# Delta rule in a streaming encoder: decay products moved ahead, write strengths in the exponent, joining products with the identity and 32x32 tiles, more buffers and banks

## The chip, the cores and the metric

The kernel runs on one core of one Trainium2 chip. The metric is the device time of one execution in microseconds (us), the median of several runs. A smaller number is better.

## The reference

One inference step of a two-layer encoder over 2048 prompt tokens and 32 sample tokens (model width 1024, all float32). Layer one is a gated delta rule with 8 heads of 128; layer two is windowed attention, which the change does not touch. What matters here is the delta rule in blocks of c tokens:

```python
gcum = jnp.cumsum(gb, axis=-1)
decay = jnp.exp(jnp.where(incl, gcum[..., :, None] - gcum[..., None, :], -jnp.inf))
kbeta = kc * bc[..., None]
lower = jnp.where(strict, jnp.einsum('nbhik,nbhjk->nbhij', kbeta, kc) * decay, 0.0)
tmat = lower + jnp.eye(c, dtype=lower.dtype)
u = lax.linalg.triangular_solve(tmat, vc * bc[..., None], left_side=True, lower=True, unit_diagonal=True)
w = lax.linalg.triangular_solve(tmat, kbeta * jnp.exp(gcum)[..., None], left_side=True, lower=True,
                                unit_diagonal=True)
intra = jnp.einsum('nbhik,nbhjk->nbhij', qc, kc) * decay
...
v_new = ui - jnp.einsum('bhck,bhkv->bhcv', wi, s)
o = jnp.einsum('bhck,bhkv->bhcv', qd, s) + jnp.einsum('bhij,bhjv->bhiv', ai, v_new)
s = s * gl[..., None, None] + jnp.einsum('bhck,bhcv->bhkv', kd, v_new)
```

The output o is normalised per head, multiplied by a gate from z, projected by `a_w_out`, added to the input and layer-normalised.

## The kernel before

The engines are TensorE (PE, with PEld for its weight loads), VectorE (DVE), ScalarE (ACT) and GpSimd (POOL); transfers are issued by SyncE (SP) and a few by ACT. Tokens lie in 5 blocks of 416. The stages follow each other:

- **P1** projects the tokens to q, k and v (each float32 product as three passes over high and low parts), applies the short convolution, and stores q, k, v and the running sums of the decay (`gcum`) in scratch memory. `gates` and `norms` make small tables for each token and head: `cc` (write strength times a norm), `ekd`, `egl`, `hn`, `rq` and `ngc` (minus the running sum).
- **Delta.run** walks over 17 chunks: 16 of 128 tokens and one of the 32 sample tokens. In between it gives PE other work in small portions (`fill`): the remaining blocks of the gate z while i is under 7, and the first tiles of the output projection once i is 15.
- **O1** projects 17 tiles of up to 128 tokens with `a_w_out`; `second.rest()` does what is left of them after the chunks. Then come **P2** (projections of layer two) and **Attention**.

In iteration i of Delta.run four chunks are in work: `ch` (chunk i), `nx` (i+1), `n2` (i+2) and `n3` (i+3). The steps of a chunk, each a generator that is advanced piece by piece:

- `load`: SP fetches `gb` (the running sums spread over all partitions), `k`, `q`, `v`, and later `z`, each in two halves of four heads. `gb` has four buffers, that is two chunks' worth, so `gb` of n3 is written over that of nx.
- `decays` (of n3): DVE adds the causal mask to `gb` (E, line 417), ACT takes eight exponentials (L423), DVE multiplies by `cc` (L427).
- `lower` (of n2): PE forms k times k (tile `g`, L441), DVE multiplies by E (`npr`), ACT gathers the 32x32 diagonal blocks, DVE transposes them into `L` (L451).
- `chain`: forward substitution inside the 32x32 blocks, 31 steps of one multiplication (tile `tm`, L462) and one subtraction (`Tt`, L465). Steps 0 to 23 run on POOL one iteration ahead, the rest on DVE (`SPLIT = 24`).
- `spread` and `invert` (of nx): DVE transposes the result, ACT spreads it into `t32` and `u32`, and five small products with copies between them (all called `bps`, in one PSUM bank) join the 32x32 inverses to a 128x128 one, `u`. The fourth product (L575) needs `ta`, which DVE makes from the third (L571).
- `turn_k`, `turn_v`, `inside`: transposes of k and v, and q times k times E. `inside` also lets ACT turn `gb` into powers (L507).
- `fade` (of nx): DVE multiplies the two halves of k, and then of q, by those powers (L516). After it `gb` of nx is free.
- `errors`, `changes`, `seen`, `advance`: k times state S (`ks`), `u` times the error (`vp`, copied to `vs`), the output (`op`), and the new state (`sp`, then S on DVE, L638).
- `squares`, `norms`, `scale`, `emit`: the normalisation, the transpose `otr`, and the product with z that is stored as `s_g`.

Within `Delta.run` the order on PE, DVE and ACT is that of the code (`tc.manual_schedule`). The order on SP and POOL, and that of all engines outside it, is set by the framework's planner. Each engine works strictly in its order, so an instruction that waits holds all behind it. In `second.rest()` only PE's order is that of the code.

Of the kernel before, what the change touches and what calls it, by code (L numbers as in the profile page):

```python
# [10 lines left out]
F32 = mybir.dt.float32  # L11
# [84 lines left out]
class P1:  # L96
# [49 lines left out]
    def qkv(self):  # L146
        nc, I, T, G, big, one = self.nc, self.I, self.T, self.G, self.big, self.one
        gtmp = one.tile([128, 8, NTT, H], F32, tag="gtmp", name="gtmp")
        abT = gtmp[:, 0:2].rearrange("p a t h -> p (a t h)").rearrange("p (t c) -> p t c", c=16)
# [97 lines left out]
def gates(nc, I, T, G, abT, gtmp, one, pt):  # L247
# [28 lines left out]
    V.reciprocal(out=G["cc"][:], in_=w)  # L276
# [27 lines left out]

def norms(nc, G, parts, sel, kind, one, pt):
# [17 lines left out]
    V.tensor_tensor(out=G["cc"][:], in0=G["cc"][:], in1=xv, op=ALU.mult)  # L323
    V.tensor_tensor(out=G["ekd"][:], in0=G["ekd"][:], in1=G["cc"][:], op=ALU.mult)
# [32 lines left out]
class Delta:  # L357
# [3 lines left out]
    SPLIT = 24  # L361

    def __init__(self, tc, es, I, O, T, G):
# [15 lines left out]
        self.f = {}  # L379
        for k in ("t32", "u32", "m1"):  # L380
            self.f[k] = one.tile([128, 8, 64], F32, tag=k, name=k)
        nc.gpsimd.memset(self.f["m1"][:], 0.0)
# [6 lines left out]
        self.S = one.tile([128, 8, 128], F32, tag="Sp", name="Sp")  # L389
        nc.gpsimd.memset(self.S[:], 0.0)  # L390
# [19 lines left out]
    def decays(self, ch):  # L410
# [13 lines left out]
        yield  # L424
        for q in range(2):
            E = ch.E[q]
            V.tensor_tensor(out=E[:n, :, :n], in0=E[:n, :, :n], in1=self.bc(G["cc"][:n, ti, q * 4:q * 4 + 4], n, n),  # L427
                            op=ALU.mult)
            yield

    def lower(self, ch):
# [4 lines left out]
        nb = self.sml.tile([128, 8, 32], F32, tag="y1", name="nb")  # L436
# [58 lines left out]
    def inside(self, ch):  # L495
# [3 lines left out]
        for q in range(2):  # L499
# [19 lines left out]
    def corners(self, ch):  # L519
        m1, npr = self.f["m1"], ch.npr  # L520
        self.nc.scalar.copy(m1[0:32, :, 32:64], npr[0:32, :, 32:64])
        self.nc.scalar.copy(m1[64:96, :, 32:64], npr[64:96, :, 96:128])

    def spread(self, ch):

        nc, V = self.nc, self.nc.vector
        n = ch.n
        sml = self.sml
        both = sml.tile([128, 2, 8, 32], F32, tag="ta", name="tcp")
        tcf, ucp = both[:, 0], both[:, 1]  # L530
        V.transpose(tcf[:n].rearrange("q p (c d) -> q c d p", d=4), ch.Tt[:n].rearrange("q i c -> q c i"))
        V.transpose(ucp[:n], tcf[:n])
        if n == 32:
            V.tensor_copy(self.u[:32, :, :32], ucp[:32])
            return
        t32, u32 = self.f["t32"], self.f["u32"]
        for dst, src in ((t32, tcf), (u32, ucp)):
            for c in range(2):
                nc.scalar.activation(dst[:, :, 32 * c:32 * c + 32], src[:], AF.Copy, scale=self.sides[:, c:c + 1])

    def invert(self, ch):
# [5 lines left out]
        t32, u32, m1, npr = self.f["t32"], self.f["u32"], self.f["m1"], ch.npr  # L547
        halves = (slice(0, 64), slice(64, 128))

        def new():  # L550
            return self.pb.tile([128, 8, 64], F32, tag="tr", name="bps")

        y1p = new()
# [10 lines left out]
        for hv in halves:  # L564
            V.tensor_tensor(out=u[hv, :, hv], in0=u32[hv], in1=up[hv], op=ALU.subtract)
        yield
        tp = new()
# [978 lines left out]
```

## Time and profile before

| What | Value |
|---|---|
| median of 3 runs | 2457.42 us (2456.83 to 2467.69) |
| profiled execution, its own time | 2461.63 us |
| its span | 2459.8 us |
| PE busy | 2251.2 us (92%) |
| DVE busy | 1441.0 us (59%) |
| ACT busy | 875.9 us (36%) |
| POOL busy | 781.3 us (32%) |
| Delta.run with its neighbours | from about 700 to 1380 us in the span |

The page gives one profiled execution. Busy shares are averages over stages that differ: PE is near 100% in P1, P2 and Attention, and lower in the chunk loop. The stage is read by windows, by the waits in it, and by the instructions in order of time.

### The profile page before, as it was taken

How to read it: one execution, taken by the hardware profiler on the slowest of the kernel's cores; microseconds unless marked ns; L12 is line 12 of the kernel's file. 1: busy time of each engine (PE TensorE's matmuls, PEld its weight loads, DVE VectorE, ACT ScalarE, POOL GpSimd, SP SyncE). 2: the span in 40 equal slices, each digit the busy share in tenths (PEclk: the TensorE clock that was granted, in tenths of full speed). 3: DMA queues.
4: the chain of work that ended last, by engine and by line, in shares of the span. 5: the costliest groups of instructions: out<-in, count | busy, mean ns of one | idle time of the engine just before them, and what ended most of it. 6: DMA issues, size and time to landing. Idle time of an engine off the chain costs nothing.

```text
span 2459.8 us, 36690 instructions
## 1 busy us (share of the span) xinstructions
PE 2251.2 (92%) x13778; PEld 2052.3 (83%) x13778; DVE 1441.0 (59%) x2883; ACT 875.9 (36%) x2133; POOL 781.3 (32%) x1184
## 2 busy tenths in 40 slices
PE   8999999999988888687777899999999998999997
PEld 6999999999977777576676677899999996777885
DVE  3775666544356667687675677622444225767875
ACT  3444344233124445355453211131111225544541
POOL 1422222111104353444452011012434123565653
PEclk9999999999988888888888999999999999999999
DMA  4121212212253443554432566442212247333321
GB/s 177 61 79 70 74 65 73 75 61 97 92 126 81 94 100 92 132 124 118 91 84 71 150 196 190 122 132 87 73 66 74 73 121 183 110 96 94 95 74 56
DMA packets 268592, 247.78 MB, mean 101 GB/s; under 512 B 67600, under 2 KB 243792, under 8 KB 265072
## 3 DMA queue, kind: packets, MB, share of 16 engines
q1 hardware_dynamic: 259456, 233.70, 32.8%
q10 hardware_dynamic: 8960, 11.76, 1.5%
q8 instruction: 108, 1.77, 0.3%
q14 instruction: 68, 0.56, 0.1%
HBM read 154.57 MB, written 91.20 MB: 100 GB/s over the span
## 4 chain that ended last, share of the span: by engine, by line
PE 72%; DMA 10%; DVE 10%; ACT 3%; issue 2%; POOL 1%; SPq 0%; DVEq 0%; ACTq 0%; POOLq 0%
PE ps L77 15%; PE ps L79 15%; PE ps L78 14%; DMA gb<-s_gcum 5%; PE ot L1286 3%; PE po L1171 2%; PE po L1172 2%; PE po L1173 2%; PE S L1265 2%; PE po L877 2%; PE po L879 2%; PE po L878 2%; DMA act_raw<-s_hT 1%; PE tr L1280 1%; PE g L441 1%
## 5 line engine op out<-in xcount | busy, mean ns | idle before, releaser
L77 PE MATMUL ps<-act_hi,w_hi 128*128 128x416 f32 x2000 | 714.9, 358 | 4.1 <-ACT act_hi L68 2.4
L79 PE MATMUL ps<-act_hi,w_lo 128*128 128x416 f32 x2000 | 706.4, 354 | 0.6 <-DVE w_lo L54 0.6
L78 PE MATMUL ps<-act_lo,w_hi 128*128 128x416 f32 x2000 | 705.4, 353 | 0.0
L77 PEld LDWEIGHTS ps<-act_hi,w_hi 128*128 128x128 f32 x2000 | 379.0, 190 | 10.8 <-ACT act_hi L68 3.8
L79 PEld LDWEIGHTS ps<-act_hi,w_lo 128*128 128x128 f32 x2000 | 379.1, 190 | 7.1 <-DVE w_lo L54 1.2
L78 PEld LDWEIGHTS ps<-act_lo,w_hi 128*128 128x128 f32 x2000 | 379.9, 190 | 4.3 <-issue 0.4
L54 POOL TENSOR_TENSOR w_lo<-w_raw,w_hi 128x1024 fp32r<-128x1024 f32 x55 | 144.6, 2630 | 656.3 <-ACT w_hi L53 646.4
L188 DVE SCALAR_TENSOR_TENSOR y<-R,convw,y 128x2083 f32<-128x2083 f32 x72 | 171.6, 2384 | 121.1 <-ACT y L186 119.8
L462 POOL TENSOR_TENSOR tm<-L,Tt 128x60 f32<-128x60 f32 (+21 forms) x384 | 125.4, 327 | 325.9 <-DVE tm L462 207.6
L1273 POOL TENSOR_TENSOR P<-P,sm 128x384 f32<-128x384 f32 (+2 forms) x128 | 104.6, 839 | 158.6 <-DVE sm L1150 86.6
L465 POOL TENSOR_TENSOR Tt<-Tt,tm 128x60 f32<-128x60 f32 (+21 forms) x384 | 140.3, 365 | 30.1
L1146 ACT ACTIVATE P<-S,nm 128x192 f32<-128x192 f32 (+2 forms) x260 | 105.0, 421 | 88.2 <-DVE nm L1139 41.4
L218 ACT COPY R<-ps 128x416 f32<-128x416 f32 (+1 forms) x144 | 61.5, 450 | 209.4 <-PE ps L79 184.3
L53 ACT CAST w_hi<-w_raw 128x1024 fp32r<-128x1024 f32 x62 | 65.0, 1049 | 178.0 <-PE ps L78 147.2
L1011 POOL TENSOR_TENSOR rs<-rs,sin 128x416 f32<-128x416 f32 x50 | 71.0, 1420 | 149.8 <-DVE rs L1010 102.3
L877 PE MATMUL po<-wo_hi,g_hi 128*128 128x512 f32 (+1 forms) x272 | 113.5, 417 | 2.0 <-ACT g_hi L863 1.2
L879 PE MATMUL po<-wo_hi,g_lo 128*128 128x512 f32 (+1 forms) x272 | 109.8, 404 | 3.4 <-DVE g_lo L864 3.4
L878 PE MATMUL po<-wo_lo,g_hi 128*128 128x512 f32 (+1 forms) x272 | 109.2, 401 | 0.0
L575 PE MATMUL bps<-ta,npr 64*64 64x64 f32 x256 | 29.0, 297 | 83.3 <-DVE ta L571 83.3
L1286 PE MATMUL ot<-pt,vd 128*128 128x256 f32 x372 | 98.6, 391 | 3.7 <-DVE graw L1289 1.6
L1171 PE MATMUL po<-wo_hi,g_hi 128*128 128x512 f32 x240 | 99.7, 415 | 0.1
L1172 PE MATMUL po<-wo_lo,g_hi 128*128 128x512 f32 x240 | 96.5, 402 | 2.6 <-DVE wo_lo L824 2.5
(266 smaller groups left out, 4168.1 us busy)
## 6 DMA issues: line engine op xcount, KB each, us to landing
w_raw<-in_w_in SPq DMA_DIRECT2D x40, 512.0 KB
w_raw<-in_b_w_in SPq DMA_DIRECT2D x20, 512.0 KB
s_z<-z SPq DMA_DIRECT2D x40, 208.0 KB
s_bz<-za SPq DMA_DIRECT2D x40, 208.0 KB
s_bq<-ra SPq DMA_DIRECT2D x40, 208.0 KB
s_q<-y SPq DMA_DIRECT2D x8, 1024.0 KB
s_k<-y SPq DMA_DIRECT2D x8, 1024.0 KB
s_v<-y SPq DMA_DIRECT2D x8, 1024.0 KB
```

Source lines behind the costliest of these rows:

```text
L54: sub.tensor_tensor(out=lo[:], in0=raw[:], in1=hi[:], op=ALU.subtract)
L77: nc.tensor.matmul(ps, hi[:, k, :], xh[:, k, :], start=(k == 0), stop=False)
L78: nc.tensor.matmul(ps, hi[:, k, :], xl[:, k, :], start=False, stop=False)
L79: nc.tensor.matmul(ps, lo[:, k, :], xh[:, k, :], start=False, stop=(k == KC - 1))
L188: nc.vector.scalar_tensor_tensor(out=y[:], in0=R[:, j:j + W], scalar=self.convw[:, i, j:j + 1], in1=y[:], op0=ALU.mult, op1=ALU.add)
L465: P.tensor_tensor(out=Tt[:n, i0:, :w], in0=Tt[:n, i0:, :w], in1=tm[:n, i0 - k:, :w], op=ALU.subtract)
L877: nc.tensor.matmul(ps[:n], ghi[:, k, :n], w[0][:, k, cs], start=(k == 0), stop=False)
L878: nc.tensor.matmul(ps[:n], ghi[:, k, :n], w[1][:, k, cs], start=False, stop=False)
L879: nc.tensor.matmul(ps[:n], glo[:, k, :n], w[0][:, k, cs], start=False, stop=(k == KC - 1))
L1171: nc.tensor.matmul(ps[:n], ghi[:, k, :n], w[0][:, k, cs], start=(k == 0), stop=False)
L1172: nc.tensor.matmul(ps[:n], ghi[:, k, :n], w[1][:, k, cs], start=False, stop=False)
L1286: nc.tensor.matmul(ot[:, p], self.vd[:, kc0 + j, p, :], pt[:, 2 * j:2 * j + 2, :], start=(j == 0), stop=(j == nj - 1))
```

## The change

It has these parts:

1. **Write strength in the exponent.** `add_log` computes the logarithm of `cc` in 20 small DVE instructions at the end of the norms of k, and adds it to `ngc`. The exponential of `decays` then holds the factor, and the two multiplications L427 for each chunk go.
2. **Decay products moved ahead.** The powers become a generator of their own (`powers`), and `fade` of nx runs from the end of iteration i-1 into the start of iteration i, before POOL's chain is started. `gb` of n3 is requested behind it as before. `decays` of n3 is advanced in smaller pieces.
3. **Joining products.** `corners` and `t32` go. The first product is 32x32 on the blocks themselves; `y1` is a fixed tile with the identity on its diagonal, so that the second and third products need no addition or subtraction. Product three comes before product two, and their banks alternate between the pools `pa` and `pb`. `ta` is copied by ACT; `u` is copied half by ACT, half by DVE.
4. **Split.** POOL does steps 0 to 24 of a full chunk (25 of 31), and 10 for the sample chunk.
5. **Buffers.** The state S becomes two tiles of four heads; q has five buffers and the v/z tiles three. For the sample chunk the stored state is loaded ahead into buffers of `gb` instead of into S after S was stored. `triu`, `ones` and `cc` live in P1's pools only.
6. **Output weights.** The low parts of `a_w_out` are made by POOL instead of DVE (`wo_lo`), one piece in each iteration from i = 8 on, instead of two.
7. **Planner.** `second.rest()` now keeps the code's order on DVE too.

```diff
+def add_log(nc, out, x, one, n, w):
...
+    V.tensor_scalar(out=ei, in0=xi, scalar1=23, scalar2=None, op0=ALU.logical_shift_right)
+    V.tensor_scalar(out=mi, in0=xi, scalar1=0x7FFFFF, scalar2=0x3F800000, op0=ALU.bitwise_and, op1=ALU.bitwise_or)
...
+    V.tensor_tensor(out=out, in0=out, in1=r[:], op=ALU.add)
...
-    SPLIT = 24
+    @staticmethod
+    def split(ch):
+        return 25 if ch.n == 128 else 10
...
-        pool, tag, bufs = (self.sml, "vz", 2) if name in "vz" else (self.four, name, 4)
+        pool, tag, bufs = (self.sml, "vz", 3) if name in "vz" else (self.four, name, 5 if name == "q" else 4)
...
             nc.scalar.activation(E, E, AF.Exp, bias=G["ngc"][:n, ti, h:h + 1])
-        yield
-        for q in range(2):
-            E = ch.E[q]
-            V.tensor_tensor(out=E[:n, :, :n], in0=E[:n, :, :n], in1=self.bc(G["cc"][:n, ti, q * 4:q * 4 + 4], n, n),
-                            op=ALU.mult)
-            yield
+            if h % 4 == 3:
+                yield
...
-            eg = ch.gb[q][:, :, :n]
-            nc.scalar.activation(eg, eg, AF.Exp)
...
+    def powers(self, ch):
+
+        for gb in ch.gb:
+            eg = gb[:, :, :ch.n]
+            self.nc.scalar.activation(eg, eg, AF.Exp)
+        yield
...
         for p in range(8):
-            for hv in halves:
-                nc.tensor.matmul(y1p[hv, p, :], m1[hv, p, :], t32[hv, p, :], start=True, stop=True)
-        y1 = sml.tile([128, 8, 64], F32, tag="y1", name="y1")
-        nc.scalar.copy(y1[:], y1p[:])
+            for r in (0, 64):
+                s, t = slice(r, r + 32), slice(r + 32, r + 64)
+                nc.tensor.matmul(y1p[t, p, 0:32], npr[s, p, t], ch.tcf[s, p, :], start=True, stop=True)
+        for r in (slice(32, 64), slice(96, 128)):
+            nc.scalar.mul(y1[r, :, 0:32], y1p[r, :, 0:32], -1.0)
         yield
-        up = new()
+        tp = new(self.pa)
+        for p in range(8):
+            nc.tensor.matmul(tp[:64, p, :], u32[:64, p, :], y1[:64, p, :], start=True, stop=True)
+        ta = sml.tile([128, 8, 64], F32, tag="ta", name="ta")
+        nc.scalar.copy(ta[:64], tp[:64])
+        yield
+        up = new(self.pb)
...
-        for hv in halves:
-            V.tensor_tensor(out=u[hv, :, hv], in0=u32[hv], in1=up[hv], op=ALU.subtract)
+        nc.scalar.copy(u[0:64, :, 0:64], up[0:64])
+        V.tensor_copy(u[64:128, :, 64:128], up[64:128])
...
-            go(z, low, low)
+            go(low, x, low)
             if n2:
                 self.load(n2, "v", (0,))
-            go(vp, vp, x, x, t, t, t, t, low, z, t, t, low)
+            go(vp, vp, z, x, z, x, low, t, t, low, t)
             if n2:
-                drain(self.chain(n2, P, 0, self.SPLIT))
+                drain(self.chain(n2, P, 0, self.split(n2)))
             if n3:
                 self.load(n3, "gb")
+            elif n2:
+                S = self.sampled()
...
+            if i > 7:
+                side()
+            if i == len(chunks) - 3:
+                side()
...
-                self.between(ch)
+                self.save("p_delta")
+                self.S = S
...
-            go(w, e, x, x)
+            go(w, e)
...
-            go(v, r, r, r, g, r, r, r, v, d, r, d, r)
+            p = gen(self.powers, n2)
+            go(v, r, r, r, g, r, r, v, r, k, r, d, v, w, r, d, p)
...
-            go(d, d, o)
-            side()
+            go(o)
             fill(more)
-            go(v, o)
+            go(v, o, d)
             z, x = self.emit(ch), gen(self.fade, n2)
+            go(x)
...
-        nc.vector.tensor_tensor(out=lo[:, k, :], in0=raws[k][:], in1=hi[:, k, :], op=ALU.subtract)
+        nc.gpsimd.tensor_tensor(out=lo[:, k, :], in0=raws[k][:], in1=hi[:, k, :], op=ALU.subtract)
...
-    with tc.manual_schedule(engines={ET.PE}):
+    with tc.manual_schedule(engines={ET.PE, ET.DVE}):
         second.rest()
```

What the change does to the order is shown at three places, in an iteration without filler work (i from 8 on).

On DVE before, from the fades of q to the first mask addition of n3 (at: q times k times E; Xo, ro_y and ro_t: the normalisation in small steps; u: the second joining product):

```order
L516 TENSOR_TENSOR q<-q,gb 128x512 x2
L505 TENSOR_TENSOR at<-gq,E 128x512
L654 TENSOR_TENSOR Xo<-Xo,t_rq 128x8
L656 SCALAR_TENSOR_TENSOR Xo<-Xo,t_rq 128x8
L658 TENSOR_SCALAR Xo<-Xo 128x8
L505 TENSOR_TENSOR at<-gq,E 128x512
L331 TENSOR_SCALAR ro_y<-Xo 128x8
L334 TENSOR_SCALAR ro_y<-ro_y 128x8
L338 SCALAR_TENSOR_TENSOR ro_t<-Xo,ro_y 128x8
L565 TENSOR_TENSOR u<-u_5060,bps 64x8x64 x2
L417 TENSOR_TENSOR E<-gb,nm 128x512
```

The first E comes here nine rows behind the fades that its buffer waits for.

On DVE after, the start of the iteration: the fades of nx alternate with `npr` of n2 and the z products, and stand ahead of the transpose L that starts POOL's chain.

```order
L550 TENSOR_TENSOR k<-k,gb 128x512
L471 TENSOR_TENSOR npr<-g,E 128x512
L550 TENSOR_TENSOR k<-k,gb 128x512
L471 TENSOR_TENSOR npr<-g,E 128x512
L709 TENSOR_TENSOR z<-otr,z 128x512
L550 TENSOR_TENSOR q<-q,gb 128x512
L709 TENSOR_TENSOR z<-otr,z 128x512
L550 TENSOR_TENSOR q<-q,gb 128x512
L491 TENSOR_TENSOR tm<-L,Tt 128x6x7
L494 TENSOR_TENSOR Tt<-Tt,tm 128x6x7
L480 STREAM_TRANSPOSE L<-nb 128x1024
```

The four fades moved from the middle of the previous iteration to this place.

And on DVE after, the place of the mask additions of the same iteration:

```order
L369 TENSOR_TENSOR ro_t<-ro_t,ro_y 128x8
L450 TENSOR_TENSOR E<-gb,nm 128x512
L599 COPY u<-bps 64x8x64
L519 TENSOR_TENSOR vn<-vtr,t_hn 128x512
L371 SCALAR_TENSOR_TENSOR ro_y<-ro_t,ro_y 128x8
L450 TENSOR_TENSOR E<-gb,nm 128x512
```

Between the last fade of q and the first E stood nine rows before; now 29 stand there (rows of the change's own list, with groups of four counted once), `ta` is gone from behind E, and one copy of u stands behind the first E.

On SP before, one iteration: `gb` stands behind both loads of k and the first of z; it overwrites what the fades of q read.

```order
L681 DMA s_g<-z 128x4x128
L407 DMA v<-s_v 128x4x128
L681 DMA s_g<-z 128x4x128
L407 DMA v<-s_v 128x4x128
L407 DMA q<-s_q 128x4x128
L407 DMA k<-s_k 128x4x128
L407 DMA z<-s_z 128x4x128
L407 DMA k<-s_k 128x4x128
L405 DMA gb<-s_gcum 128x4x128 x2
L407 DMA z<-s_z 128x4x128
```

The request is one row with both halves, and `z` waits behind it.

On SP after, `gb` follows the stores of the previous chunk's output, ahead of the loads of v, z, q and k of the iteration; a load of `a_w_out` stands between the halves of k.

```order
L710 DMA s_g<-z 128x4x128
L438 DMA gb<-s_gcum 128x4x128
L710 DMA s_g<-z 128x4x128
L438 DMA gb<-s_gcum 128x4x128
L440 DMA v<-s_v 128x4x128
L440 DMA z<-s_z 128x4x128
L440 DMA q<-s_q 128x4x128
L440 DMA k<-s_k 128x4x128
L862 DMA wo_raw<-in_a_w_out 128x1024
L440 DMA z<-s_z 128x4x128
L440 DMA k<-s_k 128x4x128
```

Both halves of `gb` moved ahead of six loads that used to stand before or among them.

On POOL before, the chain of one chunk ends and the next begins directly:

```order
L462 TENSOR_TENSOR tm<-L,Tt 128x8x6
L465 TENSOR_TENSOR Tt<-Tt,tm 128x8x6
L462 TENSOR_TENSOR tm<-L,Tt 128x31
L465 TENSOR_TENSOR Tt<-Tt,tm 128x31
L462 TENSOR_TENSOR tm<-L,Tt 128x30
L465 TENSOR_TENSOR Tt<-Tt,tm 128x30
```

Nothing else stands between the two chains.

On POOL after, from i = 8 on, a low part of `a_w_out` stands behind the first step of the chain:

```order
L491 TENSOR_TENSOR tm<-L,Tt 128x7x7
L494 TENSOR_TENSOR Tt<-Tt,tm 128x7x7
L491 TENSOR_TENSOR tm<-L,Tt 128x31
L494 TENSOR_TENSOR Tt<-Tt,tm 128x31
L869 TENSOR_TENSOR wo_lo<-wo_raw,wo_hi 128x1024
L491 TENSOR_TENSOR tm<-L,Tt 128x30
```

What moved there: a piece of work that DVE did between two chunks now stands inside POOL's chain, ahead of 24 of its steps.

More of the change, by code (lines that the diff above doesn't have):

```diff
@@ L147, in qkv @@
         nc, I, T, G, big, one = self.nc, self.I, self.T, self.G, self.big, self.one
+        G["triu"] = one.tile([128, 128], F32, tag="triu", name="triu")
+        nc.sync.dma_start(G["triu"][:], I["triu"])
+        G["ones"] = one.tile([128, 128], F32, tag="ones", name="ones")
+        nc.gpsimd.memset(G["ones"][:], 1.0)
         gtmp = one.tile([128, 8, NTT, H], F32, tag="gtmp", name="gtmp")
+        G["cc"] = gtmp[:, 3]
         abT = gtmp[:, 0:2].rearrange("p a t h -> p (a t h)").rearrange("p (t c) -> p t c", c=16)
@@ L378, in __init__ @@
         nc.sync.dma_start(self.tinit[:], I["tinit"])
[L379 to L382, printed above, removed]
+        self.u32 = one.tile([128, 8, 64], F32, tag="u32", name="u32")
         self.sides = one.tile([128, 2], F32, tag="sides", name="sides")
@@ L388, in __init__ @@
         nc.gpsimd.memset(self.u[:], 0.0)
-        self.S = one.tile([128, 8, 128], F32, tag="Sp", name="Sp")
-        nc.gpsimd.memset(self.S[:], 0.0)
+        self.y1 = one.tile([128, 8, 64], F32, tag="y1", name="y1")
+        nc.gpsimd.memset(self.y1[:], 0.0)
+        for hv in (slice(0, 64), slice(64, 128)):
+            nc.gpsimd.tensor_copy(self.y1[hv], G["ident"][hv, hv].unsqueeze(1).to_broadcast([64, 8, 64]))
+        self.S = [one.tile([128, 4, 128], F32, tag=f"Sp{q}", name="Sp") for q in range(2)]
+        for S in self.S:
+            nc.gpsimd.memset(S[:], 0.0)
     @staticmethod
@@ L535, in spread @@
             return
[L536 to L539, printed above, removed]
+        for c in range(2):
+            nc.scalar.activation(self.u32[:, :, 32 * c:32 * c + 32], ucp[:], AF.Copy, scale=self.sides[:, c:c + 1])
     def invert(self, ch):
@@ L577, in invert @@
         yield
-        u2p = new()
+        u2p = new(self.pb)
         for p in range(8):
@@ L1336, in side @@
             next(o1[0].on.rest, None)
-            next(o1[0].on.rest, None)
     def outputs():
@@ L1414, in make_consts @@
     G = {}
[L1415 to L1420 removed]
+    G["ident"] = pool.tile([128, 128], F32, tag="ident", name="ident")
+    nc.sync.dma_start(G["ident"][:], I["ident"])
+    for name in ("hn", "rq", "ekd", "egl", "ngc"):
         G[name] = pool.tile([128, NTT, H], F32, tag=name, name="t_" + name)
```

107 lines of the change are left out of this document (58 added, 49 removed).

## Prediction

> **What bounds the kernel now.** The page first, then the chunk loop in windows (columns: length; busy time and count of PE, PEld, DVE, ACT, POOL; granted TensorE clock, 1.00 being full; DMA share; GB/s). The marks are the starts of the join's fourth product, L575, in the iterations i = 0, 7, 14 and 15.
>
> ```profile
> span 2459.8 us, 36690 instructions
> PE 2251.2 (92%) x13778; PEld 2052.3 (83%) x13778; DVE 1441.0 (59%) x2883; ACT 875.9 (36%) x2133; POOL 781.3 (32%) x1184
> PEclk9999999999988888888888999999999999999999
> ```
> ```profile
> 768.06:1045.36 277.30, 215.06 (x1965) 200.99 (x1965) 186.27 (x459) 126.76 (x382) 120.75 (x346) 0.85 0.43 103
> 1045.36:1284.61 239.25, 181.51 (x1737) 168.58 (x1737) 179.17 (x450) 123.69 (x372) 111.09 (x326) 0.85 0.45 107
> 1284.61:1309.99 25.38, 22.59 (x249) 20.57 (x249) 20.82 (x63) 12.34 (x41) 14.96 (x41) 0.87 0.20 51
> ```
>
> PE is busy 92% of the span. Inside the loop (slices 12 to 22 of the last row of the first fence, the granted clock in tenths) no engine is full, and the clock is low. So seven early iterations (with filler) take 39.6 us each, seven late ones 34.2. What ended the waits between 700 and 1500 us (who waited, for whom; total, times, longest; the first row is POOL's idle time between two chains, which I come back to):
>
> ```profile
> POOL tm L462 <- DVE tm L462: 207.6, 13, 24.5
> DVE E L417 <- DMA gb<-s_gcum: 85.5, 27, 11.5
> PE bps L575 <- DVE ta L571: 83.3, 14, 14.2
> PE ks L590 <- DMA Sp<-in_state_delta: 6.3, 1, 6.3
> ```
>
> One late iteration in order of time joins the second row to the third:
>
> ```profile
> 1206.40 1.44 DVE L516 TENSOR_TENSOR q<-q,gb 128x512 f32<-128x512 f32 x2
> 1207.14 2.22 SPq L405 DMA_DIRECT2D gb<-s_gcum  x2
> 1215.82 0.78 DVE L417 TENSOR_TENSOR E<-gb,nm 128x512 f32<-128x512 f32 x1 [4.31 <-DMA gb<-s_gcum]
> 1218.59 0.67 DVE L571 TENSOR_TENSOR ta<-t,bps 64x512 f32<-64x512 f32 x1
> 1219.31 1.97 PE L575 MATMUL bps<-ta,npr 64*64 64x64 f32 x16 [5.46 <-DVE ta L571]
> 1225.05 3.58 PE L441 MATMUL g<-k 128*128 128x128 f32 x16
> 1228.47 1.95 PE L601 MATMUL vp<-vn,u 128*128 128x128 f32 x16
> ```
>
> The fades of q free `gb`, its refill is issued within 1 us and lands 8 to 10 us later. DVE stands at E meanwhile, `ta` stands behind E, and PE pauses 5.5 us. The chain that ended last says the same of this stretch:
>
> ```profile
> 1207.91 8.95 DMA gb<-s_gcum
> 1216.88 0.85 DVE E L417
> ```
>
> The pause costs more than its length. In the iteration before mark 926.96 the clock reads
>
> ```profile
> 887.00:892.00 5.00, 4.77 (x26) 0.50 0.04 11
> 892.00:897.00 5.00, 5.00 (x26) 0.50 0.00 0
> 897.00:902.00 5.00, 5.00 (x43) 0.96 0.22 62
> ```
>
> that is, half speed for about 9.5 us after the pause: some 4.5 us of work lost. In the late rows above, 16 products of L441 take 3.58 us and 16 of the same size of L601, later, 1.95.
>
> **The change, part by part.**
>
> *Fades ahead, `gb` earlier.* Before, nine DVE rows lie between the last fade and the first E (about 4 us at the 0.2 to 0.7 us of these rows), against a landing of 8 to 10 us. After, 29 rows lie between; thirteen chain steps of 0.2, L with 1.95, seven products of full width at 0.7 and the update of S come to about 12 us (the last by estimate from the others), to which comes what DVE waits for PE. Both `gb` loads also stand ahead of the loads of v, z, q and k on SP, which lie an iteration or more before their use. I take the wait as gone but for 1 us an early iteration; the ends are 0 and 2.5. What is moved costs nothing new: four fades of 0.7 us, two exponentials, the same two DMAs. They now stand ahead of L, so POOL's start could slip by their 2.8 us; I let that count only in POOL's loop below. `ta` becomes an ACT copy, ahead of the exponentials of n3 on ACT, so a late E no longer holds it; it would hold `u` and the next `vs`, which stand behind the first exponentials.
>
> Early iterations: in 277.3 us PE waited 7 times for `ta` (45.7 us in the waits of that window) and lost 7 × 4.5 = 31.5 at half clock. Without both 200.1 are left, 28.6 each, nearly all PE work, as the filler fills. Add 7 × 1 for what is left of the wait and 4 for i = 6, where the pause was 14.2:
>
> ```profile
> PE bps L575 <- DVE ta L571: 45.7, 7, 14.2
> ```
>
> There the code loads 2 MB of tables and weights at once (two of 128 x 1024 floats and two raw weights, 0.5 MB each), and that stays. So 211, a gain of 66. Ends: 200 and 228 (2.5 us each, and the clock low in every other iteration).
>
> *Late iterations: POOL is late next.* Without pause and cold work PE's 181.5 us fall to 150 (21.4 each). But POOL's chain closes a loop: DVE's first own step needs POOL's last; that step and its subtraction, then L, then POOL's next chain.
>
> ```profile
> 1198.17 1.95 DVE L451 STREAM_TRANSPOSE L<-nb 128x1024 f32<-128x1024 f32 x1 [0.52 <-ACT nb L446]
> 1200.29 0.26 POOL L462 TENSOR_TENSOR tm<-L,Tt 128x31 f32<-128x31 f32 x1 [16.70 <-DVE tm L462]
> 1206.60 0.69 POOL L465 TENSOR_TENSOR Tt<-Tt,tm 128x69 f32<-128x69 f32 x1
> 1208.07 0.35 POOL L465 TENSOR_TENSOR Tt<-Tt,tm 128x66 f32<-128x66 f32 x1
> 1219.91 0.30 POOL L465 TENSOR_TENSOR Tt<-Tt,tm 128x48 f32<-128x48 f32 x1
> 1230.48 0.20 DVE L462 TENSOR_TENSOR tm<-L,Tt 128x49 f32<-128x49 f32 x1
> L54 POOL TENSOR_TENSOR w_lo<-w_raw,w_hi 128x1024 fp32r<-128x1024 f32 x9 | 22.7, 2519 | 136.3 <-ACT w_hi L53 136.3
> ```
>
> From 1200.29 to 1220.21 are 24 steps: 0.83 us each. DVE took the result at 1230.48, so before there were 10 us to spare. After: 25 steps 20.8, L 1.95, a first step 0.4, hand-overs 0.3: 23.4. A POOL step beside a fade of q took 0.69 where its like took 0.35; four fades and their neighbours would add about 1.4: 24.8. The low part of `a_w_out` stands inside the chain for i = 8 to 13 and does not exist on POOL before; its nearest row, the same operation and size on `w_lo`, is 2.52 us: 27.3. So 24.8 + 6 × 27.3 = 188.6 for the seven, a gain of 50.6. Ends: 172 (no collisions, the low part at half its price: 23.4 + 6 × 24.7) and 203 (29 each: the pause gone, the clock still low).
>
> The low part adds a wait, too: the load of the next raw weight now needs POOL's subtraction, one step and 2.5 us into the chain, where it needed DVE's of 1.2. Behind it on SP stand the second halves of z and k, and v and q, for chunks an iteration on: 0.
>
> *i = 14* has no `gb` to wait for and took 25.38 already: near the loop's time, 1 us gained. It is also the check on the late sum: an iteration without this wait does run in 25 us.
>
> *Products with the identity, the exponent.* These go on DVE for each chunk: two multiplications L427, `ta`, one of two `u`, one chain step:
>
> ```profile
> L427 DVE TENSOR_TENSOR E<-E,t_cc 128x512 f32<-128x512 f32 (+1 forms) x34 | 21.5, 665 | 2.0 <-ACT E L423 2.0
> L571 DVE TENSOR_TENSOR ta<-t,bps 64x512 f32<-64x512 f32 x16 | 10.7, 671 | 0.5 <-PE bps L569 0.5
> L565 DVE TENSOR_TENSOR u<-u,bps 64x512 f32<-64x512 f32 x32 | 21.8, 683 | 1.8 <-PE bps L563 1.6
> ```
>
> 1.3 + 0.7 + 0.7 + 0.4 = 3.1 us, off DVE's 25.6 of a late iteration (179.2 / 7). That leaves 22.5 of 27.3, cover by POOL's loop; without the removal DVE would be within 2 us of the bound. In the sum by itself: 0. ACT gets copies of `ta` and half of `u`, each like
>
> ```profile
> L576 ACT COPY ta<-bps 64x512 f32<-64x512 f32 x16 | 9.3, 581 | 42.8 <-PE bps L575 42.8
> ```
>
> and has 17.7 us of work in a late iteration (123.7 / 7), so 19 of 27: 0. `add_log`'s 20 small instructions cost DVE 20 × 0.2 = 4 us in P1 (the price of a small step, above), where PE is full and DVE is not: 0, at worst 4.
>
> *Sample state ahead.* PE waited 6.31 us for it. I take 8, with part of a slow stretch behind it; the ends are 6 and 10.8, the wait alone and with 4.5 us of lost clock.
>
> ```profile
> 1340.35 1.03 PE L590 MATMUL ks<-Sp,k 128*32 128x128 f32 x4 [6.31 <-DMA Sp<-in_state_delta]
> ```
>
> *Buffers, the chain of the sample chunk (21 steps on DVE, beside output-projection work), the code's order on DVE in `second.rest()`:* 0, with 5 us either way for the last: DVE's low parts and remainders of the output projection now stand in one fixed order, so one that waits for PE holds the next tile's.
>
> **Sum**: 2461.6 (profiled execution) − 66 − 50.6 − 1 − 8 = 2336. The median of the runs lies 4.2 below that execution, so 2332.
>
> **A rule on the clock.** The row: after 5.46 us of pause L575 ran at 1.97, but in i = 14, after only 1.76,
>
> ```profile
> 1284.61 1.14 PE L575 MATMUL bps<-ta,npr 64*64 64x64 f32 x16 [1.76 <-DVE ta L571]
> 1290.41 3.42 PE L601 MATMUL vp<-vn,u 128*128 128x128 f32 x16
> ```
>
> it ran at 1.14 and L601, later, at 3.42. The Trainium skill, "TensorE: Matmul & The Clock Gate", Part 1, halves the clock after one idle window of about 3.4 us; by that iterations without a pause of that length would be warm, and the sum stands. The second row speaks against so sharp a limit: half speed came although no pause of 3.4 us lay close before. If PE stays cold 9.5 us of every late iteration, and that takes 29 us for 27, the sum would be 14 us more, 2346.
>
> **Rivals.**
>
> (1) The forecast: pause gone, POOL the late bound.
>
> (2) `gb` lands late still. For it: the longest wait was 11.5 us behind a landing of 4 us more, so some landings took 15; and v, z, q and k are now asked for right behind it and share the DMA engines. A pause of 2 to 3 us stays in most iterations, half speed behind it: 33 us for 30 early, 32 for 27 late, 7 × 3 + 7 × 5 = 56 more: 2388. Against it: DVE's 12 us of rows, which wait for PE as well.
>
> (3) POOL's loop is shorter: the collisions are those of the fades alone and the low part hides while POOL would wait; 25 us late and 28.6 early: 2461.6 − 77 − 64 − 1 − 8 − 4.2 = 2307.
>
> (4) The change does not do what it says: another transfer, k or v at its buffer, takes the pause over. Only this row speaks for it, three waits in the whole loop:
>
> ```profile
> PE g L441 <- DMA k<-s_k: 8.2, 3, 5.3
> ```
>
> All but the sample state's gain would be lost: about 2450.
>
> (5) Slower, by POOL alone: the steps run at the collision's 0.69, since a DVE without pauses works beside them all the time. Of a step's 0.83 us the two instructions are 0.33 and 0.37 on the mean:
>
> ```profile
> L462 POOL TENSOR_TENSOR tm<-L,Tt 128x60 f32<-128x60 f32 (+21 forms) x384 | 125.4, 327 | 325.9 <-DVE tm L462 207.6
> L465 POOL TENSOR_TENSOR Tt<-Tt,tm 128x60 f32<-128x60 f32 (+21 forms) x384 | 140.3, 365 | 30.1
> ```
>
> At 0.69 each, with the remaining 0.14 between them, a step takes 1.52 and the loop 25 × 1.52 + 2.65 = 40.7, with the low part 43.2. Six late iterations at 43.2 and one at 40.7 are 300 for 239, seven early ones 285 for 277; less 9 for the rest: 2461.6 + 61 + 8 − 9 − 4.2 = 2517. It decides from a step of (34.2 − 2.65 − 2.5) / 25 = 1.16 us. Against it: 24 steps ran at 0.83 beside a DVE busy 25.6 us of 34.2. The Trainium skill, "GPSIMD Engine Reference", Specifications, has POOL share its SBUF interfaces with VectorE, in contention with DVE instructions that read two SBUF inputs; the 0.69 beside a fade agrees.
>
> **How the numbers follow.** Chances: (1) 0.62, from 2310 to 2355; (2) 0.15; (3) 0.14; (4) 0.05; (5) 0.04. The range 2298 to 2390 takes in (1), (3) and most of (2); all favourable ends together (77, 67, 1, 10.8 and 5) give 2297, all unfavourable ones without rival (2) give 2377. About 0.5% is what a measurement of this kernel can tell from no change. Faster takes in (1) to (3) and a part of the rest: 0.92; same, most of (4): 0.04; slower: 0.04.
>
> **What would show it.** Right: E's wait for `gb` under 15 us in all; PE's wait for `ta` gone; clock above 0.93 in early windows; periods of about 30 and 27 us; POOL nearly without idle time between chains for i = 8 to 13, its low part 2.5 us; no wait of ks for `Sp`. Wrong, if `E` still waits over 2 us an iteration, if DVE instead of POOL is what the late chain runs through, or if POOL's chain takes over 25 us.

## The result and the profile after

The changed kernel took 2335.4 us (median; 2333.5 to 2340.2) where the kernel before took 2459.4 in the same comparison: a ratio of 0.949 with a 95% interval of 0.947 to 0.952. The forecast was 2332.

The page of the kernel after, the rows that answer to the first fence of the prediction:

```profile
span 2331.7 us, 36681 instructions
PE 2211.3 (95%) x13778; PEld 2014.4 (86%) x13778; DVE 1416.6 (61%) x2818; ACT 867.2 (37%) x2117; POOL 830.9 (36%) x1205
PEclk9999999999997999989988999999999999999999
```

The same product of the join is now L603; its starts in i = 0, 7, 14 and 15 bound these windows (columns as before). The product of mark i belongs to chunk i and is made late in iteration i - 1, in both kernels; "i = 7" in the rows below is the stretch from mark 7 to mark 8.

```profile
764.55:966.63 202.08, 192.65 (x1957) 179.92 (x1957) 166.23 (x413) 120.69 (x367) 124.20 (x342) 0.99 0.55 124
966.63:1162.98 196.35, 166.23 (x1738) 152.82 (x1737) 161.46 (x399) 118.74 (x364) 140.55 (x352) 0.91 0.59 139
1162.98:1193.22 30.24, 23.94 (x249) 21.02 (x249) 22.92 (x56) 16.07 (x51) 19.93 (x46) 0.77 0.34 95
```

Early iterations take 28.9 us (39.6 before), with PE busy 95% at a clock of 0.99; late ones take 28.0 (34.2 before). The waits between 700 and 1500 us:

```profile
POOL tm L491 <- DVE tm L491: 64.4, 12, 12.5
PE ks L618 <- DVE Sp L667: 27.9, 14, 3.1
PE g L470 <- DMA k<-s_k: 13.6, 4, 5.6
DVE E L450 <- DMA gb<-s_gcum: 11.2, 2, 9.9
```

E's wait for `gb` fell from 85.5 us in 27 cases to 11.2 in two, the wait of the fourth product for `ta` is gone, and PE now waits most for the new state S. Where the last third of the time lies is read from the last product of the output projection, before (L879) and after (L924), in the views of that line:

```profile
L879 PE MATMUL po<-wo_hi,g_lo x272: 388/389/795, 1321.4 to 1580.6; 128*128 128x512 f32 x128, 128*32 128x512 f32 x8
```
```profile
L924 PE MATMUL po<-wo_hi,g_lo x272: 387/389/628, 1204.3 to 1445.9; 128*128 128x512 f32 x128, 128*32 128x512 f32 x8
```

| Stretch | before | after | moved | forecast |
|---|---|---|---|---|
| start to i = 0 | 768.1 | 764.6 | -3.5 | 0 |
| i = 0 to 6 | 277.3 | 202.1 | -75.2 | -66 |
| i = 7 to 13 | 239.3 | 196.4 | -42.9 | -50.6 |
| i = 14 | 25.4 | 30.2 | +4.9 | -1 |
| i = 15 to the last output product | 270.6 | 252.7 | -17.9 | -8 |
| the rest | 879.2 | 885.8 | +6.6 | 0 |
| span | 2459.8 | 2331.7 | -128.1 | -125.6 |

The sum came out within 3 us, but its terms did not: they are off by -3.5, -9.2, +7.7, +5.9, -9.9 and +6.6 us (measured less forecast, in the order of the table), and these errors cancel. That the median lies within 4 us of the forecast is luck.

### The profile page after: what moved, and what is told of

It reads as the page before. It is cut to its first block, busy times and chain, and to the rows that moved or that the text cites. A ratio compares the mean times of both kernels' runs of the same rounds, so it can differ in the third digit from the quotient of the medians.

```text
span 2331.7 us, 36681 instructions
## 1 busy us (share of the span) xinstructions
PE 2211.3 (95%) x13778; PEld 2014.4 (86%) x13778; DVE 1416.6 (61%) x2818; ACT 867.2 (37%) x2117; POOL 830.9 (36%) x1205
## 4 chain that ended last, share of the span: by engine, by line
PE 78%; DVE 7%; POOL 6%; DMA 4%; issue 3%; ACT 2%; SPq 1%; ACTq 0%; DVEq 0%; POOLq 0%
PE ps L79 15%; PE ps L77 15%; PE ps L78 15%; PE ot L1331 3%; PE po L922 3%; PE po L924 3%; PE po L923 2%; POOL tm L491 2%; POOL Tt L494 2%; PE po L1216 2%; PE po L1217 2%; PE po L1218 2%; PE S L1310 2%; PE tr L1325 1%; DMA k<-s_k 1%
## 5 line engine op out<-in xcount | busy, mean ns | idle before, releaser
L491 POOL TENSOR_TENSOR tm<-L,Tt 128x60 f32<-128x60 f32 (+20 forms) x385 | 135.8, 353 | 167.8 <-DVE tm L491 64.4
L494 POOL TENSOR_TENSOR Tt<-Tt,tm 128x60 f32<-128x60 f32 (+20 forms) x385 | 143.5, 373 | 30.1
L924 PE MATMUL po<-wo_hi,g_lo 128*128 128x512 f32 (+1 forms) x272 | 108.3, 398 | 2.2 <-DVE g_lo L909 2.2
L1218 PE MATMUL po<-wo_hi,g_lo 128*128 128x512 f32 x240 | 96.2, 401 | 0.0
```

The costliest lines, as they stand in the source:

```text
L491: P.tensor_tensor(out=tm[:n, i0 - k:, :w], in0=L[:n, i0:, j:j + 1].to_broadcast(sh), in1=Tt[:n, j:j + 1, :w].to_broadcast(sh), op=ALU.mult)
L494: P.tensor_tensor(out=Tt[:n, i0:, :w], in0=Tt[:n, i0:, :w], in1=tm[:n, i0 - k:, :w], op=ALU.subtract)
L924: nc.tensor.matmul(ps[:n], glo[:, k, :n], w[0][:, k, cs], start=False, stop=(k == KC - 1))
```

## The experiments

Ratios are to the kernel before of the same comparison; the kernel after stands at 0.9493 (0.9465 to 0.9521), and 0.001 is 2.5 us. The first four are about the early `gb`.

**The fades of q late again.**

```diff
-            go(vp, vp, z, x, z, x, low, t, t, low, t)
+            go(vp, vp, z, z, low, t, t, low, t)
...
-            go(w, e)
+            go(w, e, x, x)
```

> The kernel after, with only the fades of q put back behind the spread, where they stood before; gb of n3 is thereby requested late again. Theory (the place of the fades carries the gain): E waits for gb about 4 us in each of 14 iterations again, u on DVE stands behind the first E, PE pauses some 4 us and works at half clock behind it: about 8 us an iteration, 2335 + 14 x 8 = 2447, at least 2420. Rival (taking ta off DVE is what freed PE): E may wait, but PE does not, and the time stays under 2360.

2377.9 us, 0.9685 (0.9671 to 0.9699): 47 us of the 124, neither theory. Its waits:

```profile
DVE E L450 <- DMA gb<-s_gcum: 78.5, 22, 9.6
PE tr L504 <- DVE vn L519: 20.9, 10, 5.1
```

`gb` is as late as before the change, and DVE stands as long. But PE stands only 21 us for it: what it waits for is no longer behind E.

**The same, and `ta` made by DVE behind the first E.**

```diff
-        nc.scalar.copy(ta[:64], tp[:64])
+        V.tensor_copy(ta[:64], tp[:64])
...
-            go(v, r, r, r, g, r, r, v, r, k, r, d, v, w, r, d, p)
+            go(v, r, r, r, g, r, r, d, v, r, k, r, d, v, w, r, p)
```

> The kernel after with the fades of q late (that kernel took 2378) and, besides, ta copied by DVE behind the first mask addition E, as it stood before. Theory (with gb late, ACT's ta is what kept E's 78 us of waiting from PE): the pause of PE ahead of its fourth product comes back, 3 to 5 us in most iterations with half speed behind it: 2420 to 2445. Rival (DVE's lighter load, not the place of ta, is the difference): 2378 to 2390.

2431.5 us, 0.9894 (0.9868 to 0.992): 51 us more than with the late fades alone, by the ratios, as the theory had it.

```profile
DVE E L450 <- DMA gb<-s_gcum: 83.3, 23, 9.7
PE vtr L518 <- DVE ta L592: 40.4, 12, 5.2
```

E waits nearly as long in both. The difference is who stands behind it. PE's pause stands ahead of `vtr`, the transpose of v, which takes a bank of the pool that the third product is copied out of as `ta`; it was expected ahead of the fourth product. The edit changes two things, the engine of `ta` and the place of E (both `d` stand earlier), so the 51 us are the price of both together. So two parts of the change each stop the same pause: `gb` earlier, and `ta` out of E's way. What `ta` behind E would cost while `gb` is early was not tried.

**The kernel before, with the fades alone moved.** 

```diff
+        go(x)
...
-            go(z, low, low)
+            go(low, x, low)
...
-            go(vp, vp, x, x, t, t, t, t, low, z, t, t, low)
+            go(vp, vp, z, x, z, x, low, t, t, t, t, t, t, low)
...
-            go(w, e, x, x)
+            go(w, e)
...
             z, x = self.emit(ch), gen(self.fade, n2)
+            go(x)
```

> The kernel before with only the fades moved to the start of the iteration, ahead of POOL's chain; the joining products, the multiplications by cc, 24 steps on POOL and the low parts of the weights on DVE stay as before. Theory: nearly the whole gain comes with it: early iterations 29 to 30 us, late ones 26 to 28, 2345 to 2370. Rival (the move needs the lighter DVE): DVE, with 25.6 us of work in a late iteration, becomes the bound or ta is late on DVE, and 2400 to 2430 is left.

2429.1 us, 0.9895 (0.9879 to 0.9911): only 26 us, so the theory fell. The time lies in the rival's range, but not by the rival's mechanism: PE's wait for `ta` is 7.9 us where it was 83.3, and no wait for DVE is near that for v.

```profile
DVE E L417 <- DMA gb<-s_gcum: 10.6, 2, 9.5
PE vtr L489 <- DMA v<-s_v: 60.1, 13, 7.0
PE bps L575 <- DVE ta L571: 7.9, 12, 1.2
```

The wait for `gb` is gone as in the kernel after; a wait for v, 4.6 us in each of 13 iterations, has taken its place.

**The kernel after with two v/z buffers.**

```diff
-        pool, tag, bufs = (self.sml, "vz", 3) if name in "vz" else ...
+        pool, tag, bufs = (self.sml, "vz", 2) if name in "vz" else ...
```

> The kernel after with two buffers instead of three for the v and z tiles. Theory (from the run with the fades alone moved, where PE waited 60 us for v): the third buffer is what lets the early gb pay; without it v comes some 4 us late in most iterations, and with the clock behind that the time rises by 50 to 80 us, to 2390 to 2420 where the kernel after would take about 2333. Rival (the wait for v came from the old order of z and the loads, not from the buffers): at most 10 us more.

2391.3 us, 0.9736 (0.9718 to 0.9755): 60 us more, as the theory had it. The wait and, on SP's queue, what it comes from:

```profile
PE vtr L518 <- DMA v<-s_v: 67.2, 13, 7.7
```
```profile
984.06 7.62 SPq L440 DMA_DIRECT2D v<-s_v  x2
```

The two halves of v take SP 7.6 us, most of it waiting. Between 700 and 1400 us SP's loads at L440 wait 110.7 us, in 28 cases, for PE's transposes of v, which free such a buffer (67.4 us in 18 cases with three buffers); so it is the buffer that holds v. With the third one (2 KB in each partition) PE's wait for v is not among the waits. The third buffer together with the early fades in the kernel before was not tried, so that these two alone would bring the gain there is not shown.

**The multiplications by `cc` back on DVE**, before the next fade of k, without the logarithm.

```diff
+        for q in range(2):
+            E = ch.E[q]
+            V.tensor_tensor(out=E..., in0=E..., in1=self.bc(G["cc"]...), op=ALU.mult)
+            yield
...
-            go(x)
+            go(d, d, x)
```

> The kernel after with the two multiplications by cc back on DVE (behind the exponentials, ahead of the next fade of k) and without the logarithm. Theory A (DVE's work is hidden under PE early and under POOL late): 0 to 4 us more. Theory B (any delay on DVE between the fades and the spread reaches PE as a pause, and the clock makes it dear): 1.3 us in every iteration and some cold stretches, 20 to 40 us more.

2346.9 us, 0.9559 (0.9542 to 0.9576): 16 us more, between the two theories. The windows of its early and late iterations:

```profile
764.50:968.93 204.43, 193.83 (x1957) 180.13 (x1957) 175.35 (x427) 120.77 (x367) 129.72 (x343) 0.99 0.53 120
968.93:1174.52 205.59, 168.24 (x1737) 151.88 (x1737) 171.30 (x414) 119.66 (x365) 150.66 (x365) 0.93 0.57 135
```

Early it is 2 us, hidden under PE as forecast; late it is 9 us. Of these about 1 us an iteration is steady (i = 9 to 12 take 28.0 us on the mean, 26.8 in the kernel after); the rest lies in single stretches, as i = 13 with 32.4 us at a clock of 0.79. The reading for the steady part, which no run isolates, is that DVE's work between two POOL chains is not hidden, since it stands ahead of the L that starts the next one.

**22 chain steps on POOL.**

```diff
-        return 25 if ch.n == 128 else 10
+        return 22 if ch.n == 128 else 10
```

> The kernel after with 22 instead of 25 chain steps of a full chunk on POOL and nine instead of six on DVE. Theory (POOL's loop is the late bound): the loop loses 3 x 0.83 = 2.5 us, late iterations come to 25 us, 10 to 14 us less: about 2323; early ones unchanged, since PE fills them. Rival (DVE's own steps lie on PE's path through the spread and the joining products): 3 x 0.4 = 1.2 us more in every iteration, 2335 to 2350.

2364.5 us, 0.9634 (0.9614 to 0.9655): 35 us more, outside both ranges. The rival was right on the path and too low on the price. PE's wait for the spread, the first product of the join in one early iteration, and the clock behind it:

```profile
PE bps L584 <- DVE tcp L560: 21.1, 15, 1.9
```
```profile
886.40 0.69 PE L584 MATMUL bps<-tcp,npr 32*32 32x32 f32 x32 [1.84 <-DVE tcp L560]
```
```profile
890.00:896.20 6.20, 6.20 (x52) 0.54 0.10 28
```

The three steps more on DVE make PE wait 1.4 us at a time, 21 in all, and half speed follows some of these pauses.

**The low parts of the output weights on DVE again.**

```diff
-        nc.gpsimd.tensor_tensor(out=lo[:, k, :], in0=raws[k][:], in1=hi[:, k, :], op=ALU.subtract)
+        nc.vector.tensor_tensor(out=lo[:, k, :], in0=raws[k][:], in1=hi[:, k, :], op=ALU.subtract)
```

> The kernel after, with the low parts of the output weights made by DVE again instead of POOL. Theory (POOL's chain bounds i = 8 to 13, and the 2.35 us of that piece stand in it): periods of 25 instead of 26.9 there, and i = 14 without the two pieces and without DVE's subtraction of 4.17 us beside them 4 to 5 us shorter: about 15 us less, 2320. Rival (DVE is as near to the bound): its 1.2 us more cost the same, 2330 to 2337.

2315.4 us, 0.9437 (0.942 to 0.9453): 14 us less than the kernel after, the fastest kernel here, and the size of the theory. But only a part is POOL's chain. Its late window, and the last output product:

```profile
965.26:1154.17 188.91, 164.32 (x1737) 151.04 (x1737) 158.49 (x405) 118.67 (x364) 133.01 (x348) 0.93 0.61 144
```
```profile
L924 PE MATMUL po<-wo_hi,g_lo x272: 387/389/796, 1193.2 to 1435.6; 128*128 128x512 f32 x128, 128*32 128x512 f32 x8
```

The late iterations are 7.4 us shorter, i = 14 is 2.2 shorter, and behind the output projection the span has 878.0 us left (2313.6 - 1435.6) where the kernel after has 885.8. The first of these numbers is soft: the last two runs below have the same code in the late iterations as the kernel after, and their traces show 192.2 and 193.4 us for its 196.4, so 3 to 7 us is what can be said. The last number is firm: in the traces of all kernels here the rest takes 878.0 to 879.4 us with the low parts on DVE and 885.8 to 890.6 with them on POOL. The function that makes the low parts serves layer two as well: its eight pieces, too, had moved to POOL, beside Attention. There the sums of `sm` on DVE, in the kernel after and with the low parts on DVE:

```profile
L1194 DVE TENSOR_TENSOR sm<-sm,es 128x4 f32<-128x4 f32 (+1 forms) x66 | 24.7, 374 | 48.8 <-ACT P L1191 27.1 <-ACT es L1193 20.2 <-POOL wo_lo L869 0.7
```
```profile
L1194 DVE TENSOR_TENSOR sm<-sm,es 128x4 f32<-128x4 f32 (+1 forms) x66 | 12.8, 195 | 32.4 <-ACT es L1193 17.7 <-ACT P L1191 11.9 <-POOL P L1318 1.8
```

**The same, with 26 steps on POOL.**

```diff
-        return 25 if ch.n == 128 else 10
+        return 26 if ch.n == 128 else 10
```

> The low parts on DVE as before (that kernel took 2315), and 26 instead of 25 chain steps on POOL. Theory (POOL's chain is the late bound with 25 steps already): a step of 0.83 us more in seven or eight late iterations, about 2321. Rival (DVE's own steps lie on PE's way to the joining products, as 22 steps on POOL showed with 33 us more): the spread comes 0.4 us earlier, PE pauses less, 2305 to 2312.

2320.9 us, 0.9447 (0.9431 to 0.9463). The median is that of the theory (2321), but by the ratios it is 2.5 us more than 25 steps, and the intervals overlap: the time alone does not tell the two apart. The trace does: in each, four late iterations take nearly the same, 26.7 to 27.0 us here and 26.0 to 26.1 with 25 steps, which is the 0.83 us of a step. The late window:

```profile
963.56:1158.22 194.66, 165.98 (x1738) 153.09 (x1737) 156.01 (x391) 118.76 (x364) 137.82 (x364) 0.91 0.59 143
```

With 22 steps DVE's share is late for PE, with 26 POOL's is late for DVE.

**The low parts on DVE and the layer-norm tables loaded later** (in iterations 11 and 12).

```diff
         if k + 2 < KC:
             load(k + 2)
+        if 3 <= k < 3 + len(tabs):
+            nc.sync.dma_start(tabs[k - 3][0][:], tabs[k - 3][1].partition_broadcast(128))
```

> The low parts on DVE, and the two layer-norm tables (0.5 MB each) loaded in iterations 11 and 12 instead of at the change from i = 6 to 7. Theory (k is late by 5 us in i = 7 because of 2 MB and more asked for at once): the wait of k goes, i = 7 takes 26 instead of 29.3 us: 2311 where the kernel without this took 2315. Rival (the weights alone, or what the tables do later, keep the wait): 2314 to 2318.

2320.2 us, 0.9448 (0.943 to 0.9466), no gain over 0.9437 (the intervals overlap): the rival, or a little worse. PE's wait for k in i = 7 is 4.1 us in the kernel with only the low parts on DVE, and here it is the same in two pieces:

```profile
971.98 1.13 PE L470 MATMUL g<-k 128*128 128x128 f32 x8 [1.91 <-DMA k<-s_k]
975.17 2.05 PE L470 MATMUL g<-k 128*128 128x128 f32 x8 [2.06 <-DMA k<-s_k]
```

The tables are not what holds k; which of the other transfers does was not tried.

**The low parts on DVE, and the first half of S ahead of L**, the low part behind S.

```diff
-            go(vp, vp, z, x, z, x, low, t, t, low, t)
+            go(vp, vp, z, x, z, x, low)
+            if i > 7:
+                go(seen, a)
+            go(t, t, low, t)
...
-            go(seen, a, t, t)
+            if i <= 7:
+                go(seen, a)
+            go(t, t)
...
```

> The kernel with the low parts on DVE (2315), and from i = 8 on the output with the old state and the first half of the new state S stand ahead of DVE's first chain step and of L, the low part behind S. Theory (PE's pauses of 2 us for S behind L cool the clock and make one late iteration in four 31 us instead of 26): the pauses go, all late iterations take 25 to 26, 5 to 10 us less: 2306 to 2310. Rival (S ahead of L holds POOL's chain back by 1.1 us for each chunk): 2315 to 2325.

2324.6 us, 0.946 (0.9437 to 0.9483), not better than 0.9437 (the intervals overlap). The rival's time. Two of its waits between 700 and 1400 us:

```profile
POOL tm L491 <- DVE tm L491: 81.7, 14, 12.0
PE bps L584 <- DVE tcp L560: 10.9, 10, 3.1
```

POOL's idle time between chains is 82 us where it was 66 without the edit, so S ahead of L does hold the chain back; PE's wait for S fell from 22.8 to 15.7 us, and 11 us for the spread came up.

**The sample state loaded late again.**

```diff
-            elif n2:
-                S = self.sampled()
...
-                self.S = S
+                for q in range(2): ... dma_start(self.S[q][:], ...)
```

> The kernel after with the stored state of the sample chunk loaded into S only once S has been stored, as before. Theory: ks waits 6 us for it again, with some lost clock 8 us more: about 2341 where the kernel after takes 2333. Rival (output-projection work fills the time): 0 to 2 us.

2336.2 us, 0.951 (0.9488 to 0.9533): 4 us more by the ratios, and within the intervals no difference. From i = 15 to the last output product its trace has 258.2 us for 252.7, but its late iterations, which the edit does not touch, have 4.2 less; two traces differ by as much without a cause in the code. PE's wait is 1.4 us, not 6:

```profile
1214.71 1.03 PE L618 MATMUL ks<-Sp,k 128*32 128x128 f32 x8 [1.38 <-DMA Sp<-in_state_delta]
```

**DVE's order in `second.rest()` left to the planner.**

```diff
-    with tc.manual_schedule(engines={ET.PE, ET.DVE}):
+    with tc.manual_schedule(engines={ET.PE}):
```

> The kernel after with DVE's order in the remainder of the output projection left to the planner, as before. Theory of the prediction: within 5 us of the kernel after, either way (2328 to 2338). Rival (the order in the code keeps remainders off the low parts): 6 to 15 us more.

2350.1 us, 0.9567 (0.9544 to 0.959): 18 us more, the rival's side and beyond its 15 us. PE's granted clock and busy time in 40 us of the remainder, with the code's order (the kernel after) and without:

```profile
1313.22:1353.22 40.00, 40.00 (x189) 1.00 0.76 225
```
```profile
1311.06:1351.06 40.00, 34.57 (x159) 0.96 0.64 197
```

The stretch from i = 15 to the last output product takes 267.2 us, 14.5 more. That the code's order helps by keeping remainders off the low parts, as the rival said, is not shown.

## Why the prediction was right, point by point

**The pause and its clock: right, and shown; the split was off.** E's wait is gone, PE's pause with it, and the early clock went from 0.85 to 0.99. By the two early windows PE's busy time fell by 22.4 us, where I had 31.5 for half clock, and its idle time by 52.8 (62.2 to 9.4), where I had 45.7 for the waits for `ta`: the clock was priced too high, and other small waits went too. I kept 1 us an iteration and 4 for i = 6 back; neither came. The burst moved on instead: in i = 7 PE waits 5.3 us for k, and that iteration takes 31.5 us.

**"Buffers: 0" was the step that failed most.** As a cost of its own it is nothing, but the early fades pay only with it. Undoing the fades costs 47 us, undoing the third buffer 60, and the fades alone, on the kernel before, bring 26 of 124. The rival that says so (the fourth: "k or v at its buffer" takes the pause over) had 0.05, since the trace of before showed no wait for v. It could not: with `gb` early the wait for v appears, 60 us in the run with the fades alone. That run is this rival in most of its size. The forecast came true because the change also had the buffer that its sum put at nothing.

**`ta` on ACT was right in place and not priced.** I let it ride on the fades. By the late fades with and without it, taking it out from behind E is worth 51 us while `gb` is late.

**POOL is late next: right in mechanism and size.** One chain of the kernel after, its low part, and DVE's first step behind it, which waited:

```profile
1096.37 0.26 POOL L491 TENSOR_TENSOR tm<-L,Tt 128x31 f32<-128x31 f32 x1 [2.52 <-DVE tm L491]
1096.97 2.35 POOL L869 TENSOR_TENSOR wo_lo<-wo_raw,wo_hi 128x1024 fp32r<-128x1024 f32 x1
1121.08 0.20 DVE L491 TENSOR_TENSOR tm<-L,Tt 128x42 f32<-128x42 f32 x1 [2.03 <-POOL Tt L494]
1123.54 0.26 POOL L491 TENSOR_TENSOR tm<-L,Tt 128x31 f32<-128x31 f32 x1 [2.49 <-DVE tm L491]
```

From one first step to the next are 27.17 us; I had 27.3, with 2.52 for the low part. In the chain of work that ended last, POOL's rows are 59% of the late window. The term was 7.7 us short through i = 7 (31.5, with the wait for k) and i = 8, which ran at a low clock behind pauses of PE for S of 2.37 and 1.08 us:

```profile
998.10:1029.07 30.97, 27.29 (x249) 24.91 (x248) 23.64 (x58) 17.33 (x54) 23.96 (x61) 0.78 0.61 135
```

The five iterations behind them average 26.8.

**i = 14 was mis-signed.** I gave it 1 us; it lost 4.9. Two low parts stand in that iteration, and DVE stands with them. That they are POOL's costs 2.2 us of the 4.9, by the run with them on DVE (28.0); the rest was not split. The rows:

```profile
1177.60 2.34 POOL L869 TENSOR_TENSOR wo_lo<-wo_raw,wo_hi 128x1024 fp32r<-128x1024 f32 x1
1180.12 2.33 POOL L869 TENSOR_TENSOR wo_lo<-wo_raw,wo_hi 128x1024 fp32r<-128x1024 f32 x1
```
```profile
1178.33 4.17 DVE L494 TENSOR_TENSOR Tt<-Tt,tm 128x28 f32<-128x28 f32 x1
1097.68 1.68 DVE L494 TENSOR_TENSOR Tt<-Tt,tm 128x28 f32<-128x28 f32 x1
```

A subtraction of about 0.2 us ran 4.17, ending at 1182.50 when POOL's second piece had ended at 1182.45; beside the single piece of another iteration it ran 1.68. All 17 subtractions of this size in the trace say the same: ten without a piece beside them take 0.18 to 0.21 us, six beside one 1.67 to 1.75, one beside two 4.17. The four updates of S beside the same pieces, which read one input from PSUM, keep their 0.34 us. The collision I priced on POOL's side alone; it works both ways, and the longer instruction decides the wait. The Trainium skill, "GPSIMD Engine Reference", Specifications, names the shared SBUF interfaces; these rows agree and give the price. Rival (5) did not come: POOL's chain takes (24.7 - 2.35) / 25 = 0.89 us a step, where it was 0.83.

**DVE's 3.1 us "by itself: 0"** was right early (2 us with `cc` back) and wrong late (1 us an iteration there, 9 in all), by the reading above because DVE's work from the end of one POOL chain to the next L is in POOL's loop.

**The remainder "0, 5 us either way"** was too small: the code's order is worth 18 us here. **The sample state's 8** was too large: 4 by the times, not told from 0. In the stretch of the fifth row of the table the two are 14.5 and 5.5 us by the traces, for its 17.9.

**Not in the sum at all:** the low parts of layer two, made by the same function; by the run with them on DVE some 8 us, which covers the 6.6 of "the rest" in the table. The 3.5 us ahead of i = 0 were not followed.

**Two ends were added up wrong**, without weight for the range: the early end of 228 is 231 to 236 by its own terms (200, 7 × 2.5, and 4.5 in three or four iterations), and all unfavourable ends as they are written give 2375, not 2377.

## What to carry to other kernels

Moving a load earlier paid here only when what was behind the old wait was early too: look for the buffers and queue places of the next load, since the trace of before hides them behind the wait it shows. Ask of a late transfer not only how late it is but which instructions stand behind its waiter on the same engine; taking one of them out from behind it was worth as much here (51 us) as the earlier transfer itself (47). And when a helper is changed, look for its other callers.

## What the runs showed of the hardware

Pauses well under the 5 us of the kernel before were enough for half speed. In the kernel with the low parts on DVE, i = 11 has two pauses for S, and its clock reads

```profile
1088.45 1.16 PE L618 MATMUL ks<-Sp,k 128*128 128x128 f32 x8 [2.37 <-DVE Sp L667]
1090.93 2.08 PE L618 MATMUL ks<-Sp,k 128*128 128x128 f32 x8 [0.68 <-DVE Sp L667]
```
```profile
1085.00:1090.00 5.00, 2.63 (x22) 0.97 0.59 47
1090.00:1095.00 5.00, 4.32 (x32) 0.50 0.83 232
1095.00:1100.00 5.00, 5.00 (x54) 0.50 0.94 282
1100.00:1103.50 3.50, 3.50 (x41) 0.52 0.04 12
```

so that this iteration took 30.8 us between others of 26.0 and 24.7. In the run with 22 steps on POOL a pause of 1.84 us and one of 0.36 behind it were enough (the rows shown there). In the kernel after, the same product waited longer, 2.51 us and 1.25 us for its second half, and the clock of the whole iteration stayed full:

```profile
1097.82 1.16 PE L618 MATMUL ks<-Sp,k 128*128 128x128 f32 x8 [2.51 <-DVE Sp L667]
```
```profile
1081.93:1108.50 26.57, 21.93 (x249) 20.03 (x248) 23.25 (x57) 17.08 (x53) 20.37 (x51) 1.00 0.57 133
```

The Trainium skill, "TensorE: Matmul & The Clock Gate", Part 1, asks for an idle window of about 3.4 us for half speed and as long a busy one for full speed; here 2.37 and 0.68 us with 1.8 us of work between them did it, and half speed lasted 13 us of nearly full work. The measurement decides: a pause need not last 3.4 us. What decides between two such iterations was not settled.
